# Row sums of squared differences: eight neighbouring rows on a partition, and the first load of x in two

## The chip, the cores and the metric

The kernel runs on one core of a Trainium2 chip; the other cores are idle. The metric is the device time of one execution in microseconds. "The span" of a profile is the time from its first to its last instruction, and is a little shorter than that.

The engines that matter here are VectorE (DVE in the profile), ScalarE (ACT) and SyncE (SP), whose queue issues the loads and stores. The loads themselves are carried by the core's sixteen DMA engines.

## The reference

```python
def setup_inputs():
    batch, dim = 1024, 4096
    return {
        "x": np.random.randn(batch, dim).astype(np.float32),
        "y": np.random.randn(batch, dim).astype(np.float32),
        "axis": -1,
    }

def reference(x, y, axis):
    return np.sum((x - y) ** 2, axis=axis).astype(np.float32)
```

Two arrays of 16 MiB each are read once, and 1024 sums (4 KB) are written.

## The kernel before

Each of the 128 partitions holds eight rows, 32,768 columns of x and as many of y (`N = R * D` with `R = 8`, `D = 4096`). The buffers `X` and `Y` have room for six rows, `H = 6 * D`; the last two rows go to the places of rows 0 and 1 once these are squared. Rows 0 to 3 of a partition come from the first half of the batch and rows 4 to 7 from the second.

```python
    M = N // 2
    xv = x.rearrange("(h p r) d -> p h (r d)", h=2, p=P)
    yv = y.rearrange("(h p r) d -> p h (r d)", h=2, p=P)
    ov = out.rearrange("(h p r) -> h p r", h=2, p=P)
    ...
    xw = [16384, 8192, 5472, 1280, 960, 320, 160]
    yw = [16384, 8064, 2624, 2784, 1344, 480, 480, 288]
    late, last = 128, 192
    LATE = 5
    halved = (1, 2, 3, 4)
    cut = (LATE + 1) * D - late
```

`xw` and `yw` are the widths of the loads in columns; each load moves so many columns of all 128 partitions, in one packet per partition. The loads of y leave out 128 columns at the end of row `LATE`; these come last of all, after the last 192 columns of row 7. x and y loads are put in one order, so that each load of y follows the loads of x that it needs, and SyncE's queue issues them in this order. The first two are issued ahead of the rest of the program (`prog.early`), the next ones up to the room of the buffers at once, and the others when row 1 has been squared:

```python
    todo = list(order)
    for _ in range(2):
        load(*todo.pop(0))
    prog.early(mybir.EngineType.SP)
    while todo and todo[0][5] <= H:
        load(*todo.pop(0))
```

For each load of y that has landed, VectorE subtracts piece by piece (a piece lies within one row, and the loads in `halved` are cut in two once more), and ScalarE squares and sums the piece into a column of `parts` or `results`:

```python
    def sub(c0, c1):
        a = X[:, home(c0, c1)]
        nc.vector.tensor_sub(out=a, in0=a, in1=Y[:, home(c0, c1)]).then_inc(diffs, 1)
        n["diffs"] += 1

    def square(c0, c1, acc):
        a = X[:, home(c0, c1)]
        nc.scalar.wait_ge(diffs, n["diffs"])
        nc.scalar.activation(out=a, in_=a, func=Square, accum_out=acc).then_inc(acts, 1)
        n["acts"] += 1
```

The last piece is subtracted, squared and summed on VectorE alone; its sum starts from what the rest of its row gave (`scalar`). `complete(r)` adds up the parts of row r. The first half of the results is stored once row 3 is done, the second at the end.

```python
    for j, (c0, c1) in enumerate(ys):
        final = j == len(ys) - 1
        wait_loaded(c1, landed_y[j][1])
        for piece in pieces_of(j, c0, c1):
            sub(*piece)
            r = piece[0] // D
            if final:
                nc.vector.wait_ge(diffs, n["diffs"])
                nc.vector.tensor_tensor_reduce(
                    ...
                    scalar=where[piece],
                    op0=mult,
                    op1=add,
                    accum_out=results[:, r : r + 1],
                ).then_inc(sums, 1)
                n["sums"] += 1
                continue
            square(*piece, where[piece])
            squared[piece] = n["acts"]
            if r in (0, 1):
                nc.sync.wait_ge(acts, n["acts"])
                ...                      # loads into the places of rows 0 and 1
            if r == R // 2 - 1:
                nc.sync.wait_ge(acts, n["acts"])
                nc.sync.dma_start(out=ov[0], in_=results[:, 0 : R // 2]).then_inc(stored, 16)
        if j == 4:
            for r in (4, 5, 6):
                complete(r)
            nc.vector.wait_ge(sums, n["sums"])
    complete(7)

    nc.sync.wait_ge(sums, n["sums"])
    nc.sync.dma_start(out=ov[1], in_=results[:, R // 2 : R]).then_inc(stored, 16)
```

Of the kernel before, what the change touches and what calls it, by code (L numbers as in the profile page):

```python
# [47 lines left out]
def kernel(tc, x, y, axis, out):  # L48
    nc = tc.nc
    P = nc.NUM_PARTITIONS  # L50
    F32 = mybir.dt.float32
    Square = mybir.ActivationFunctionType.Square
    mult, add = mybir.AluOpType.mult, mybir.AluOpType.add

    B, D = x.shape
    R = B // P
    N = R * D

    M = N // 2
    xv = x.rearrange("(h p r) d -> p h (r d)", h=2, p=P)
    yv = y.rearrange("(h p r) d -> p h (r d)", h=2, p=P)
    ov = out.rearrange("(h p r) -> h p r", h=2, p=P)


    H = 6 * D
    X = nc.alloc_sbuf_tensor("X", [P, H], F32).ap()
    Y = nc.alloc_sbuf_tensor("Y", [P, H], F32).ap()
    results = nc.alloc_sbuf_tensor("results", [P, R], F32).ap()  # L70

    xw = [16384, 8192, 5472, 1280, 960, 320, 160]
    yw = [16384, 8064, 2624, 2784, 1344, 480, 480, 288]
    late, last = 128, 192
    LATE = 5
    halved = (1, 2, 3, 4)
    cut = (LATE + 1) * D - late
    assert sum(xw) == N and sum(yw) == N - late - last  # L80
    xs, c = [], 0
    for w in xw:
        xs.append((c, c + w))
        c += w
    ys, c = [], 0
    for w in yw:
        ys.append((c, c + w))
        c += w
        if c == cut:
            c += late  # L90
    ys += [(N - last, N), (cut, cut + late)]

    prog = Program(nc, tc)
    stored = nc.alloc_semaphore("stored")
    diffs = prog.semaphore("diffs")
    acts = prog.semaphore("acts")
    sums = prog.semaphore("sums")
    n = dict(diffs=0, acts=0, sums=0)

    def home(c0, c1):  # L100
        h0 = c0 % H
        return slice(h0, h0 + c1 - c0)


    landed_x, landed_y = [], []
    freed = []

    def load(landed, src, dst, name, c0, c1):
        sem = prog.semaphore("%s%d" % (name, len(landed)))
        nc.sync.dma_start(out=dst[:, home(c0, c1)], in_=src[:, c0 // M, c0 % M : c0 % M + c1 - c0]).then_inc(sem, 16)  # L110
        landed.append(((c0, c1), sem))

    order = []
    have = 0
    for c0, c1 in ys:
        while have < c1:
            order.append((landed_x, xv, X, "x") + xs[len([o for o in order if o[3] == "x"])])
            have = order[-1][5]
        order.append((landed_y, yv, Y, "y", c0, c1))
# [9 lines that stand above are left out]
    row_parts = [[] for _ in range(R)]  # L129
    def pieces_of(j, c0, c1):  # L130

        pieces = []
        while c0 < c1:
            e = min(c1, (c0 // D + 1) * D)
            if j in halved:
                h = (c0 + e) // 64 * 32
                pieces.append((c0, h))
                c0 = h
            pieces.append((c0, e))
            c0 = e  # L140
        return pieces

    for j, (c0, c1) in enumerate(ys):
        for piece in pieces_of(j, c0, c1):
            row_parts[piece[0] // D].append(piece)
    parts, where = None, {}
    total = sum(len(p) for p in row_parts if len(p) > 1)
    parts = nc.alloc_sbuf_tensor("parts", [P, total], F32).ap()
    k = 0
    for r, p in enumerate(row_parts):  # L150
        for piece in p:
            where[piece] = parts[:, k : k + 1] if len(p) > 1 else results[:, r : r + 1]
            k += len(p) > 1
    first = {}
    k = 0
    for r, p in enumerate(row_parts):
        if len(p) > 1:
            first[r] = k
            k += len(p)

    def parts_of(r, m):
        return parts[:, first[r] : first[r] + m]

    seen_x = [0]

    def wait_loaded(c1, ysem):

        waits = []
        while seen_x[0] < len(xs) and xs[seen_x[0]][0] < c1:
            waits.append(seen_x[0])  # L170
            seen_x[0] += 1
        nc.vector.wait_ge(ysem, 16)
        for k in waits:
            nc.vector.wait_ge(landed_x[k][1], 16)
# [12 lines that stand above are left out]
    squared = {}  # L187

    def complete(r):

        done = row_parts[r][:-1] if r == LATE else row_parts[r]
        nc.vector.wait_ge(acts, squared[done[-1]])
        nc.vector.tensor_reduce(  # L193
            out=where[row_parts[r][-1]] if r == LATE else results[:, r : r + 1],
            in_=parts_of(r, len(done)),
            axis=mybir.AxisListType.X,
            op=add,
        ).then_inc(sums, 1)
# [11 lines that stand above are left out]
                    out=Y[:, home(*piece)],  # L210
                    in0=X[:, home(*piece)],
                    in1=X[:, home(*piece)],
                    scale=1.0,
                    scalar=where[piece],
                    op0=mult,
                    op1=add,
                    accum_out=results[:, r : r + 1],
# [8 lines that stand above are left out]
                while todo and todo[0][5] <= H + (r + 1) * D:  # L226
                    load(*todo.pop(0))
                if r == 1:
                    while todo:
                        load(*todo.pop(0))  # L230
            if r == R // 2 - 1:

                nc.sync.wait_ge(acts, n["acts"])
                nc.sync.dma_start(out=ov[0], in_=results[:, 0 : R // 2]).then_inc(stored, 16)
        if j == 4:
            for r in (4, 5, 6):
                complete(r)
            nc.vector.wait_ge(sums, n["sums"])
    complete(7)

    nc.sync.wait_ge(sums, n["sums"])
    nc.sync.dma_start(out=ov[1], in_=results[:, R // 2 : R]).then_inc(stored, 16)
    prog.close(nc.sync, stored, 32)


# [33 lines left out]
```

## Time and profile before

| | before |
|---|---|
| time, median of 3 runs | 85.02 us (84.97 to 85.23) |
| span of the profiled execution | 83.6 us |
| VectorE busy | 36.9 us (44%) |
| ScalarE busy | 33.5 us (40%) |
| moved by the DMA engines | 33.56 MB in 2736 packets, 401 GB/s over the span |

A line of the profile that begins with a line number (L178 is the subtraction, L184 the square, L193 `complete`, L209 the last squared sum, L110 the loads, L225, L234 and L242 waits or stores on SyncE's queue) gives the engine, the operation, output<-inputs with their shapes, and a count. Idle time before an instruction is in square brackets, with what ended it. "SPq" is the issuing of DMAs by SyncE's queue; how long a transfer is under way from its issue stands in the list of DMA issues. Two things count where the engines are idle half of the time: when each load lands, and what waits for it.

### The profile page before, as it was taken

How to read it: one execution, taken by the hardware profiler on the slowest of the kernel's cores; microseconds unless marked ns; L12 is line 12 of the kernel's file. 1: busy time of each engine (PE TensorE's matmuls, PEld its weight loads, DVE VectorE, ACT ScalarE, POOL GpSimd, SP SyncE). 2: the span in 40 equal slices, each digit the busy share in tenths (PEclk: the TensorE clock that was granted, in tenths of full speed). 3: DMA queues.
4: the chain of work that ended last, by engine and by line, in shares of the span. 5: the costliest groups of instructions: out<-in, count | busy, mean ns of one | idle time of the engine just before them, and what ended most of it. 6: DMA issues, size and time to landing. Idle time of an engine off the chain costs nothing.

```text
span 83.6 us, 136 instructions
## 1 busy us (share of the span) xinstructions
DVE 36.9 (44%) x27; ACT 33.5 (40%) x41; POOL 0.2 (0%) x4
## 2 busy tenths in 40 slices
DVE  0000000000000000000399999999199995989980
ACT  0500000000000000000001979797979999799980
POOL 0000000000000000000000000000000000000000
DMA  9389999975999999299979988997999899999920
GB/s 470 157 376 501 501 501 501 501 313 219 470 501 501 501 501 439 125 439 501 439 313 501 501 359 386 494 494 324 410 429 440 371 437 433 405 421 407 388 74 1
DMA packets 2736, 33.56 MB, mean 401 GB/s; under 512 B 560, under 2 KB 1456, under 8 KB 1840
## 3 DMA queue, kind: packets, MB, share of 16 engines
q1 hardware_dynamic: 2736, 33.56, 94.9%
HBM read 33.55 MB, written 0.00 MB: 401 GB/s over the span
## 4 chain that ended last, share of the span: by engine, by line
DMA 64%; SPq 17%; DVE 12%; ACT 4%; issue 1%
DMA Y<-in_y_dram 64%; SPq L110 17%; DVE X L178 11%; ACT X L184 4%; DVE Y L209 0%; DVE results L193 0%; SPq L225 0%; DVE results L209 0%
## 5 line engine op out<-in xcount | busy, mean ns | idle before, releaser
L178 DVE TENSOR_TENSOR X<-X,Y 128x4096 f32<-128x4096 f32 (+10 forms) x21 | 36.2, 1779 | 44.5 <-DMA Y<-in_y_dram 44.3
L184 ACT ACTIVATE X<-X 128x4096 f32<-128x4096 f32 (+9 forms) x20 | 31.2, 1559 | 45.8 <-DVE X L178 45.6
L184 ACT ACTIVATION_READ_ACCUMULATOR X<-X 128x1 f32 x20 | 3.7, 186 | 0.0
L184 ACT ACT_TABLE_LOAD x1 | 1.3, 1283 | 1.9 <-PEq L19 1.9
L193 DVE TENSOR_REDUCE results<-parts 128x1 f32<-128x2 f32 (+2 forms) x3 | 0.4, 151 | 0.0
L209 DVE CUSTOM_DVE_ANT_0 Y<-X,parts 128x128 f32<-128x128 f32 x1 | 0.4, 352 | 0.0
L193 DVE TENSOR_REDUCE parts<-parts 128x1 f32<-128x2 f32 x1 | 0.1, 145 | 0.0
L260 POOL MEMSET const-bfloat16-1.0<- 128x1 bf16 x1 | 0.1, 102 | 0.0
L260 POOL MEMSET const-uint8-127<- 128x1 uint8 x1 | 0.1, 102 | 0.0
L260 POOL MEMSET const-float32-0.0<- 128x1 f32 x1 | 0.1, 99 | 0.2 <-issue 0.2
L260 POOL MEMSET const-float32-1.0<- 128x1 f32 x1 | 0.1, 99 | 0.0
L209 DVE DVE_READ_ACCUMULATOR2_ANT results<- 128x1 f32 x1 | 0.1, 84 | 0.0
## 6 DMA issues: line engine op xcount, KB each, us to landing
X<-in_x_dram SPq DMA_DIRECT2D x1, 4096.0 KB, 48.9
Y<-in_y_dram SPq DMA_DIRECT2D x1, 4032.0 KB, 58.1
X<-in_x_dram SPq DMA_DIRECT2D x1, 2736.0 KB, 13.3
Y<-in_y_dram SPq DMA_DIRECT2D x1, 1392.0 KB, 18.9
Y<-in_y_dram SPq DMA_DIRECT2D x1, 1312.0 KB, 16.0
Y<-in_y_dram SPq DMA_DIRECT2D x1, 672.0 KB, 21.0
X<-in_x_dram SPq DMA_DIRECT2D x1, 640.0 KB, 19.9
X<-in_x_dram SPq DMA_DIRECT2D x1, 480.0 KB, 21.7
```

What stands on the lines that cost most here:

```text
L110: nc.sync.dma_start(out=dst[:, home(c0, c1)], in_=src[:, c0 // M, c0 % M : c0 % M + c1 - c0]).then_inc(sem, 16)
L178: nc.vector.tensor_sub(out=a, in0=a, in1=Y[:, home(c0, c1)]).then_inc(diffs, 1)
L184: nc.scalar.activation(out=a, in_=a, func=Square, accum_out=acc).then_inc(acts, 1)
L193: nc.vector.tensor_reduce(out=where[row_parts[r][-1]] if r == LATE else results[:, r : r + 1], in_=parts_of(r, len(done)), axis=mybir.Axis ...
L209: nc.vector.tensor_tensor_reduce(out=Y[:, home(*piece)], in0=X[:, home(*piece)], in1=X[:, home(*piece)], scale=1.0, scalar=where[piece], o ...
L260: nc = _bacc.Bacc("TRN2", target_bir_lowering=False, num_devices=1)
```

## The change

The map of rows to partitions becomes the plain one: partition p holds rows 8p to 8p+7, 128 KB in one run. The first load of x is split in two, 4096 columns (16 KB of each partition) and then 12288, so that the first packets are small. With the plain map, the columns that come last are now the end of row 3, and the widths of the first two y loads follow from that; row 3 has only one other part, from which the last sum can start without a reduction. The results are stored once, at the end.

```diff
-    M = N // 2
-    xv = x.rearrange("(h p r) d -> p h (r d)", h=2, p=P)
-    yv = y.rearrange("(h p r) d -> p h (r d)", h=2, p=P)
-    ov = out.rearrange("(h p r) -> h p r", h=2, p=P)
+    xv = x.rearrange("(p r) d -> p (r d)", p=P)
+    yv = y.rearrange("(p r) d -> p (r d)", p=P)
+    ov = out.rearrange("(p r) -> p r", p=P)
...
-    xw = [16384, 8192, 5472, 1280, 960, 320, 160]
-    yw = [16384, 8064, 2624, 2784, 1344, 480, 480, 288]
+    xw = [4096, 12288, 8192, 5472, 1280, 960, 320, 160]
+    yw = [16256, 8192, 2624, 2784, 1344, 480, 480, 288]
     late, last = 128, 192
-    LATE = 5
+    LATE = 3
...
-        nc.sync.dma_start(out=dst[:, home(c0, c1)], in_=src[:, c0 // M, c0 % M : c0 % M + c1 - c0]).then_inc(sem, 16)
+        nc.sync.dma_start(out=dst[:, home(c0, c1)], in_=src[:, c0:c1]).then_inc(sem, 16)
...
     def complete(r):
-        done = row_parts[r][:-1] if r == LATE else row_parts[r]
-        nc.vector.wait_ge(acts, squared[done[-1]])
+        nc.vector.wait_ge(acts, squared[row_parts[r][-1]])
         nc.vector.tensor_reduce(
-            out=where[row_parts[r][-1]] if r == LATE else results[:, r : r + 1],
-            in_=parts_of(r, len(done)),
+            out=results[:, r : r + 1],
+            in_=parts_of(r, len(row_parts[r])),
...
-                    scalar=where[piece],
+                    scalar=parts_of(r, 1),
...
-            if r == R // 2 - 1:
-                nc.sync.wait_ge(acts, n["acts"])
-                nc.sync.dma_start(out=ov[0], in_=results[:, 0 : R // 2]).then_inc(stored, 16)
         if j == 4:
             for r in (4, 5, 6):
                 complete(r)
-            nc.vector.wait_ge(sums, n["sums"])
     complete(7)
 
     nc.sync.wait_ge(sums, n["sums"])
-    nc.sync.dma_start(out=ov[1], in_=results[:, R // 2 : R]).then_inc(stored, 16)
-    prog.close(nc.sync, stored, 32)
+    nc.sync.dma_start(out=ov, in_=results).then_inc(stored, 16)
+    prog.close(nc.sync, stored, 16)
```

## The prediction

> **What bounds the kernel now.** I read the page first: its line of busy engines, the two lines of DMA and the chain that ended last.
>
> ```profile
> span 83.6 us, 136 instructions
> DVE 36.9 (44%) x27; ACT 33.5 (40%) x41; POOL 0.2 (0%) x4
> ...
> DMA packets 2736, 33.56 MB, mean 401 GB/s; under 512 B 560, under 2 KB 1456, under 8 KB 1840
> ...
> q1 hardware_dynamic: 2736, 33.56, 94.9%
> ...
> DMA Y<-in_y_dram 64%; SPq L110 17%; DVE X L178 11%; ACT X L184 4%; DVE Y L209 0%; DVE results L193 0%; SPq L225 0%; DVE results L209 0%
> ```
>
> No compute engine is busy for half of the span, and the packets of the loads fill 94.9% of the sixteen DMA engines: 0.949 x 83.6 = 79.3 us. The work is a stream of 33.55 MB, and the kernel is that stream plus a start and a tail. Next the list of DMA issues, whose last column is the time from issue to landing (the two 8 MB loads are listed without a size).
>
> ```profile
> X<-in_x_dram SPq DMA_DIRECT2D x1, 4096.0 KB, 48.9
> Y<-in_y_dram SPq DMA_DIRECT2D x1, 4032.0 KB, 58.1
> ...
> X<-in_x_dram SPq DMA_DIRECT2D x1, 21.8
> Y<-in_y_dram SPq DMA_DIRECT2D x1, 40.7
> ```
>
> With the issue times of the timeline (0.00, 0.43, 1.92 and 2.29 us) these four land at 21.8 (x), 41.1 (y), 50.8 (x) and 60.4 us (y). They were all issued in the first 3 us and arrive in the order of issue. The rate comes from the table by stretches of time, which puts a packet into the stretch in which it starts; its last two columns are the DMA share and GB/s.
>
> ```profile
> 1.00:1.25 0.25, 0.00 (x0) 0.00 (x0) 0.00 (x0) 1.00 9.42 3146
> ...
> 28.00:29.00 1.00, 0.00 (x0) 0.00 (x0) 0.00 (x0) 1.00 2.42 1049
> 45.00:46.00 1.00, 1.00 (x2) 0.41 (x1) 0.00 (x0) 1.00 1.23 524
> ```
>
> In 28 to 29 us 1049 KB start, which is sixteen packets of 64 KB, one for each engine, and their time is 2.42 us each: 65,536 B / 2.42 us = 27.1 GB/s an engine, 433 GB/s for sixteen. At 45 us sixteen packets of 32 KB take 1.23 us each, against 1.21 for half of 2.42: an additional packet costs some 0.02 us at most. In 1.00 to 1.25 us twelve packets start and take 9.42 x 0.25 x 16 / 12 = 3.14 us each: the first packet is 0.72 us longer than later ones.
>
> A model with one constant then holds for the landings: 2.4 us + bytes of one engine / 27.1 GB/s. An engine carries eight partitions of each load, so 8 x 2.42 = 19.4 us for each of the first two and 9.7 and 9.5 us for the next two: 21.8, 41.1, 50.8, 60.3 against 21.8, 41.1, 50.8, 60.4 seen. For all bytes (2.097 MB an engine, 77.4 us) it gives 79.8 us; the last load landed at 80.30. So the thirteen smaller loads lost about 0.5 us altogether, 0.04 us each.
>
> Last the timeline of VectorE, which shows how close compute is behind the stream:
>
> ```profile
> 41.13 17.43 DVE L178 TENSOR_TENSOR X<-X,Y 128x4096 f32<-128x4096 f32 x4 [41.13 <-DMA Y<-in_y_dram]
> 60.43 8.76 DVE L178 TENSOR_TENSOR X<-X,Y 128x2048 f32<-128x2048 f32 x4 [1.87 <-DMA Y<-in_y_dram]
> 70.13 2.96 DVE L178 TENSOR_TENSOR X<-X,Y 128x1312 f32<-128x1312 f32 x2 [0.94 <-DMA Y<-in_y_dram]
> 73.46 4.80 DVE L178 TENSOR_TENSOR X<-X,Y 128x736 f32<-128x736 f32 x6 [0.37 <-DMA Y<-in_y_dram]
> ...
> 78.49 2.39 DVE L178 TENSOR_TENSOR X<-X,Y 128x480 f32<-128x480 f32 x5
> 80.92 0.35 DVE L209 CUSTOM_DVE_ANT_0 Y<-X,parts 128x128 f32<-128x128 f32 x1
> ```
>
> VectorE waits for y at every stage (1.87, 0.94 and 0.37 us), and in the last stage it still has about 0.1 us of wait before each of the last two loads. The last load sets the end: landing 80.30, two subtractions 0.57, the squared sum 0.35, the reduction of row 7, then the store, issued at 81.46 and landed 2.2 us later. Another 85.02 - 83.6 = 1.4 us lie outside the span.
>
> **What the Trainium skill says.** Three places bear on it, all in "DMA: Bandwidth & Descriptors". The section "Where 436 GB/s comes from" puts the ceiling of the sixteen ports at 435.2 GB/s; the 433 GB/s of the 64 KB packets agree, so nothing in the middle of the stream is left to win. The section "Why small descriptors are slow (HBM only)" says that each packet carries a small fixed cost; the trace agrees in that 32 KB packets take 1.23 us instead of 1.21. The section "Latency and other measured facts" reports copies between HBM tensors that slow down when the row pitch is a large power of two: 207 GB/s at a pitch of 512 KiB against 214 when padded, and half of that at 4 MiB. The change doubles a pitch that is a power of two, from 64 to 128 KB, which is still below the smallest one the page has. The trace of before has the 64 KB pitch alone and runs at the ceiling, so it can't say what 128 KB does.
>
> **The change, part by part.**
>
> 1. *The map of rows.* A partition reads eight rows in one run of 128 KB instead of two runs of 64 KB half a batch apart. Bytes and packet sizes of each load stay as they were; only HBM addresses move: neighbouring partitions are 128 KB apart. The engines' rate is at their ceiling, and I take the new pitch as neutral: 0.0 us.
>
> 2. *The first load of x in two.* One load of eight 64 KB packets an engine becomes eight of 16 KB and eight of 48 KB. That is eight data packets and one completion more on each engine. At 0.04 us for an additional load (the thirteen small ones) to 8 x 0.02 us (the difference of 32 KB packets) it costs 0.04 to 0.16 us; I take +0.1. It feeds no instruction earlier: VectorE's first subtraction needs y, which is still one load of 16,256 columns, behind all 16,384 of x.
>
> 3. *What goes out early.* The first two loads in the order are issued ahead of everything else. These are now both halves of x (8.4 MB, about 19 us of stream), and y follows about 1.9 us after the first. The stream can't run dry: 0.0 us.
>
> 4. *Which end comes last.* 128 columns of row 3, instead of row 5, wait to the end. The first y load is 128 columns shorter: 65.5 KB / 433 GB/s = 0.15 us. VectorE starts at 41.13 - 0.15 + 0.1 = 41.1 us. The second y load is 128 columns longer, so the sum up to it is the same and it lands at 60.4 + 0.1 us. There VectorE has 128 columns more: the 1984-column pieces took 2.22 us and the 2048-column ones 2.29, so two of them add 0.14 us, against a wait of 0.94 us at the next stage. None of it reaches the end.
>
> 5. *The reductions.* The last piece's squared sum starts from row 3's single partial instead of the reduction of row 5. There are still three reductions (rows 4, 5 and 6), so only the wait for their completion goes. In the timeline the third of them ends at 78.45 and the next subtraction starts at 78.49: at most 0.04 us, and VectorE then waits for a load anyway. 0.0 us.
>
> 6. *One store instead of two.* The early store of the first half was issued at 71.04 us, after the last load, and landed at 80.6. It leaves the queue behind the loads, so its going frees nothing ahead of them. The last store has 32 B a partition instead of 16, in the same number of packets: I take the same 2.2 us.
>
> Sum: 0.0 + 0.1 + 0.0 + 0.0 + 0.0 + 0.0 = +0.1 us. Against it stands the rival at the start, to which I give one chance in three of about -0.3 us, that is -0.1. Together 85.02 + 0.1 - 0.1 = 85.0 us.
>
> **The rivals.**
>
> *Smaller first packets shorten the start.* The constant of 2.4 us holds 0.72 us by which the first packets are longer. If part of that grows with the packet, as when writing begins only after much of a packet is read, 16 KB packets would save up to 0.5 us: 84.5 us. For it: the cost is there, before any engine is up to speed. Against it: the late starters in the same table begin between 1.75 and 2.25 us and end with the others, so this looks like a latency that all share, which a smaller packet doesn't lower. A gain could come through: VectorE's waits of 0.37 + 0.1 + 0.1 us in the last stages are about 0.5 us that an earlier stream can still remove.
>
> *The new pitch slows reading.* If partitions 128 KB apart fall on the same parts of the memory more often, each packet gets longer. One per cent on 77.4 us is 0.8 us: 85.8 us. For it: the pages' warning on pitches. Against it: the 64 KB pitch is a power of two as well and runs at 433 of 435 GB/s, limited by the engines.
>
> *The end of the stream.* [...]From 79 to 80 us the engines move 317 GB/s with a share of 1.03. If the last few loads get a tenth slower or faster over about 2 us, that is 0.2 us either way.
>
> *Compute takes over the end.* VectorE would have to lose more than 0.9 us in the middle. The change adds 0.14 us: 85.0 us as before.
>
> **Range and chances.** The range is 84.4 to 85.7: below it would need the whole start-up gain plus a faster end (0.5 + 0.1), above it a slow-down of the stream by nearly one per cent (0.7 of 77.4 us). Two per cent are 1.7 us. To win them would need over twice the whole 0.72 us that the first packets lose; to lose them the stream would have to run 2.2% slower everywhere, which only the pitch could do. So faster 0.02, same 0.95, slower 0.03.
>
> **What would show it right or wrong.** Right: packets again 2736 (144 more for the load, 144 fewer for the store); the first part of x landing at 2.4 + 4.8 = 7.2 us, the second near 21.8, the first y near 41.0 and the last y near 80.4; packets of 48 KB at about 1.8 us; waits of VectorE of about 1.9, 0.8 and 0.4 us. The start is refuted as neutral if all landings from x on are earlier by the same few tenths. The pitch is refuted as neutral if 64 KB packets of y take clearly more than 2.42 us, so that the delay grows from landing to landing. The prediction is wrong if either moves the last landing by over 0.6 us, or if VectorE no longer waits for the last loads.

## The result, and the profile after

The changed kernel takes 84.11 us (median of 4 runs, 83.95 to 84.14) where the kernel before takes 85.12 us (84.97 to 85.55, with one more run than in the table of before): a ratio of 0.9869, 95% interval 0.983 to 0.9909. It is faster by about 1.0 us, and lies below the range of the prediction.

The page of the changed kernel begins as that of before did; the lines below are its span, its busy engines and its packets.

```profile
span 82.8 us, 136 instructions
DVE 36.9 (45%) x27; ACT 33.5 (40%) x41; POOL 0.2 (0%) x4
...
DMA packets 2736, 33.56 MB, mean 405 GB/s; under 512 B 432, under 2 KB 1328, under 8 KB 1712
```

The busy times are the same and the packets as many. Next come three lines of the list of DMA issues, with the size and the time from issue to landing, and three of the table by stretches of time (last columns: DMA share, GB/s).

```profile
Y<-in_y_dram SPq DMA_DIRECT2D x1, 8128.0 KB, 39.1
X<-in_x_dram SPq DMA_DIRECT2D x1, 6144.0 KB, 21.3
...
X<-in_x_dram SPq DMA_DIRECT2D x1, 2048.0 KB, 7.2
```

```profile
1.00:1.25 0.25, 0.00 (x0) 0.00 (x0) 0.00 (x0) 1.00 4.19 852
...
8.00:9.00 1.00, 0.00 (x0) 0.00 (x0) 0.00 (x0) 1.00 1.81 786
...
28.00:29.00 1.00, 0.00 (x0) 0.00 (x0) 0.00 (x0) 1.00 2.40 1040
```

The two parts of x land at 7.2 and 21.8 us and y at 1.9 + 39.1 = 41.0 us. The packets of 65,024 bytes in 28 to 29 us take 2.40 us each, 27.1 GB/s an engine, as the 64 KB packets did with the old map. The first packets of 16 KB (thirteen start in 1.00 to 1.25 us) take 4.19 x 0.25 x 16 / 13 = 1.29 us, about 0.68 us more than 16 KB at that rate: nearly the 0.72 us of the 64 KB packets.

VectorE's timeline has the same waits (in brackets) as before, within 0.3 us:

```profile
40.99 17.30 DVE L176 TENSOR_TENSOR X<-X,Y 128x4096 f32<-128x4096 f32 x4 [40.99 <-DMA Y<-in_y_dram]
60.43 8.90 DVE L176 TENSOR_TENSOR X<-X,Y 128x2048 f32<-128x2048 f32 x4 [2.14 <-DMA Y<-in_y_dram]
70.07 2.96 DVE L176 TENSOR_TENSOR X<-X,Y 128x1312 f32<-128x1312 f32 x2 [0.74 <-DMA Y<-in_y_dram]
73.40 4.80 DVE L176 TENSOR_TENSOR X<-X,Y 128x736 f32<-128x736 f32 x6 [0.37 <-DMA Y<-in_y_dram]
```

So the stream hardly moved. The last thing ahead of the store is the reduction of row 7, which waits for ScalarE's square of that row's last 192 columns. It starts 0.03 us (unrounded) after ScalarE's last instruction has ended, at 81.05 + 0.18 = 81.23 us before and at 80.93 + 0.19 = 81.12 us after. The profile's chain puts the end down to the last waited-for load instead, as the prediction did; VectorE's work behind that load ended at nearly the same time. First before, then after:

```profile
81.05 0.18 ACT L184 ACTIVATION_READ_ACCUMULATOR X<-X 128x1 f32 x1
...
81.27 0.16 DVE L193 TENSOR_REDUCE results<-parts 128x1 f32<-128x8 f32 x1
```

```profile
80.93 0.19 ACT L182 ACTIVATION_READ_ACCUMULATOR X<-X 128x1 f32 x1
...
81.15 0.16 DVE L189 TENSOR_REDUCE results<-parts 128x1 f32<-128x8 f32 x1
```

And these are the last store's issue and, from the answer on its line, its time to landing; again first before, then after:

```profile
81.46 0.34 SPq L242 DMA_DIRECT2D out_dram<-results  x1
...
DMA to landing us min/median/max: 2.2/2.2/2.2
```

```profile
81.34 0.35 SPq L233 DMA_DIRECT2D out_dram<-results  x1
...
DMA to landing us min/median/max: 1.4/1.4/1.4
```

Of the 0.85 us between the profiled spans, 0.06 us are there when the subtractions of 736 columns begin (the timeline's last line, 73.46 and 73.40 us), 0.06 come from there to the store's issue (8.00 and 7.94 us), and 0.73 from the store itself (landed after 2.15 and 1.42 us). The trace has the landing of each of the sixteen engines; for four transfers these are the first and the last engine's, in us from the start. The lower two rows are two later runs, on a chip with the number 9.

```
kernel, chip            first 16384 of x   first y        last load      last store
before, first           21.23 to 21.79     40.62 to 41.10  80.13 to 80.48  82.70 to 83.61
changed, first          21.40 to 21.77     40.60 to 40.97  80.25 to 80.47  82.58 to 82.76
before, chip 9          21.36 to 21.94     40.81 to 41.31  80.15 to 80.59  82.82 to 82.99
changed, chip 9         21.35 to 21.90     40.56 to 41.09  80.08 to 80.47  82.66 to 82.83
```

In the first measurement the store of the kernel before begins to land after 1.2 us, as the others do, but its engines then come in over 0.9 us instead of 0.2.

### The profile page after: what moved, and what is told of

Read it like the earlier page. It is cut to its first block, busy times and chain, and to the rows that moved or that the text cites. A ratio compares the mean times of both kernels' runs of the same rounds, so it can differ in the third digit from the quotient of the medians.

```text
span 82.8 us, 136 instructions
## 1 busy us (share of the span) xinstructions
DVE 36.9 (45%) x27; ACT 33.5 (40%) x41; POOL 0.2 (0%) x4
## 2 busy tenths in 40 slices
DMA packets 2736, 33.56 MB, mean 405 GB/s; under 512 B 432, under 2 KB 1328, under 8 KB 1712
## 3 DMA queue, kind: packets, MB, share of 16 engines
q1 hardware_dynamic: 2736, 33.56, 96.0%
## 4 chain that ended last, share of the span: by engine, by line
DMA 63%; SPq 16%; DVE 12%; ACT 4%; issue 1%
DMA Y<-in_y_dram 63%; SPq L108 16%; DVE X L176 11%; ACT X L182 4%; DVE Y L205 0%; DVE results L189 0%; SPq L221 0%; DVE results L205 0%
## 5 line engine op out<-in xcount | busy, mean ns | idle before, releaser
L176 DVE TENSOR_TENSOR X<-X,Y 128x2048 f32<-128x2048 f32 (+10 forms) x21 | 36.2, 1779 | 44.4 <-DMA Y<-in_y_dram 44.2
L182 ACT ACTIVATE X<-X 128x2048 f32<-128x2048 f32 (+9 forms) x20 | 31.2, 1559 | 45.7 <-DVE X L176 45.7
## 6 DMA issues: line engine op xcount, KB each, us to landing
Y<-in_y_dram SPq DMA_DIRECT2D x1, 8128.0 KB, 39.1
```

## The experiments

My theory after the result was that the last store's packets of 16 bytes land later than packets of 32. The rivals: the early store into the same output slows the last one; the map or the split of x makes the gain; or the slow store belongs to the chip of that measurement. Each experiment was run beside the kernel before on one chip. The record of the first measurement doesn't name its chip; the others have numbers.

| kernel | chip | us | before there | ratio, 95% interval |
|---|---|---|---|---|
| b_store32 | 12 | 84.40 | 84.34 | 1.0011 (0.9996 to 1.0025) |
| b_noearly | 12 | 84.40 | 84.34 | 1.0014 (1.0002 to 1.0026) |
| a_store16 | 12 | 84.68 | 84.34 | 1.0048 (1.0035 to 1.006) |
| a_unsplit | 12 | 84.21 | 84.34 | 0.9989 (0.9977 to 1.0001) |
| before_again | 9 | 84.31 | 84.33 | 0.9992 (0.9982 to 1.0002) |
| after_again | 9 | 84.04 | 84.33 | 0.9965 (0.9951 to 0.9978) |
| b_split | 9 | 84.18 | 84.33 | 0.9986 (0.9977 to 0.9995) |
| before_look | 4 | 84.20 | 84.34 | one run |
| b_noearly_2 | 4 | 84.34 | 84.34 | 1.0002 (0.9993 to 1.0011) |
| a_half16 | 4 | 84.10 | 84.34 | 0.9972 (0.9963 to 0.9981) |
| a_fine | 4 | 84.36 | 84.34 | 1.0003 (0.9995 to 1.0012) |
| b_noearly_3 | 5 | 84.30 | 84.37 | 0.9995 (0.9981 to 1.0008) |
| after_3 | 7 | 84.14 | 84.34 | 0.9974 (0.9964 to 0.9983) |
| a_unsplit_2 | 7 | 84.12 | 84.34 | 0.9978 (0.9966 to 0.9989) |
| b_split_2 | 7 | 84.18 | 84.34 | 0.9986 (0.997 to 1.0003) |
| b_noearly_4 | 7 | 84.39 | 84.34 | 1.0014 (0.9993 to 1.0036) |
| a_oldmap | 9 | 84.30 | 84.34 | 0.9995 (0.998 to 1.0009) |
| a_unsplit_3 | 9 | 84.24 | 84.34 | 0.9988 (0.9979 to 0.9997) |

The kernel before needs 84.33 to 84.37 us on all five chips, 0.8 us less than in the first measurement. The changed kernel needs 84.04 and 84.14 us, as it did there.

### The last store

**One store of 32 bytes in the kernel before.** The output's order differs from the reference's here, because each partition's results go to eight neighbouring places.

```diff
-                nc.sync.dma_start(out=ov[0], in_=results[:, 0 : R // 2]).then_inc(stored, 16)
...
-    nc.sync.dma_start(out=ov[1], in_=results[:, R // 2 : R]).then_inc(stored, 16)
-    prog.close(nc.sync, stored, 32)
+    nc.sync.dma_start(out=out.rearrange("(p r) -> p r", p=P), in_=results).then_inc(stored, 16)
+    prog.close(nc.sync, stored, 16)
```

> The kernel before with one edit: both stores are replaced by one at the end, of 32 bytes per partition (each partition's eight results go to eight neighbouring places of the output, so the output's order differs from the reference's). Loads and map are those of before. If the packet size of the last store makes the difference: the store lands about 1.4 us after its issue instead of 2.2, and the time is about 84.2 us. If the split of x or the map of the loads makes it: 85.0 to 85.1 us and 2.2 us.

**No early store.** Rows 0 to 3 of each partition are not written.

```diff
-            if r == R // 2 - 1:
-                nc.sync.wait_ge(acts, n["acts"])
-                nc.sync.dma_start(out=ov[0], in_=results[:, 0 : R // 2]).then_inc(stored, 16)
...
-    prog.close(nc.sync, stored, 32)
+    prog.close(nc.sync, stored, 16)
```

> The kernel before without its early store (rows 0 to 3 of the output are not written); the last store keeps its 16 bytes per partition. If the packet size of the last store makes the difference: nothing changes, 85.0 to 85.1 us, store landing in 2.2 us. If an earlier store into the same output slows the last one: about 84.2 us and 1.4 us.

**The changed kernel's store in packets of 16 bytes.**

```diff
-    results = nc.alloc_sbuf_tensor("results", [P, R], F32).ap()
+    results = nc.alloc_sbuf_tensor("results", [P, 2 * R], F32).ap()
...
-    nc.sync.dma_start(out=ov, in_=results).then_inc(stored, 16)
+    nc.sync.dma_start(
+        out=out.rearrange("(p a b) -> p a b", p=P, a=2),
+        in_=results.rearrange("p (a b) -> p a b", a=2)[:, :, 0:4],
+    ).then_inc(stored, 16)
```

> The changed kernel with one edit: the results lie in two groups of four with a gap, so that its single store goes out in 256 packets of 16 bytes instead of 128 of 32. If the packet size makes the difference: the store takes about 2.2 us or somewhat more and the time is 84.9 to 85.1 us. If the early store, the map or the split makes it: 84.1 to 84.2 us, with the store landing in 1.4 to 1.5 us.

All three ran on chip 12. With packets of 32 bytes the time is that of the kernel before, and without the early store it is that or 0.1 us more. The store in 16-byte packets without an early one lands in 1.4 us, as its line in the list of DMA issues shows:

```profile
out_dram<-results SPq DMA_DIRECT2D x1, 2.0 KB, 1.4
```

The store of 256 packets of 16 bytes does cost something, 84.68 against 84.21 us for the changed kernel with the whole first load. Its issue and its line in the list of DMA issues:

```profile
81.37 0.62 SPq L233 DMA_DIRECT2D out_dram<-results  x1
...
out_dram<-results SPq DMA_DIRECT2D x1, 4.0 KB, 1.9
```

From issue to landing it takes 1.9 us instead of 1.4; 0.27 us of the difference are a longer issue (0.62 against 0.35 us). Its engines land within 0.2 us of each other (83.14 to 83.31), so this isn't what happened in the first measurement: twice as many packets cost it, not their size. So my theory had nothing to explain on this chip, and the next question was whether the kernel before was slow at all elsewhere.

**Both kernels unchanged, on one chip.**

> The kernel before, unchanged, to see how long its last store takes on the chip of this call. If the 2.2 us belong to the kernel (its packets of 16 bytes or its early store): again 2.2 us and a time 0.8 us over that of the changed kernel. If they belonged to the chip or the placement of that first measurement: 1.4 us here, and both kernels within 0.3 us of each other.

> The changed kernel, unchanged, on the same chip as the kernel before. If the gain belongs to the kernel: 0.9 to 1.0 us faster than before, as in the first measurement. If it came from a slow store of the kernel before on that chip alone: 0.1 to 0.3 us faster, with the store landing in 1.4 us in both.

On chip 9 the store of the kernel before takes 1.4 us. The first of these lines is from the timeline, the second from the answer on the store's line:

```profile
81.58 0.34 SPq L242 DMA_DIRECT2D out_dram<-results  x1
...
DMA to landing us min/median/max: 1.4/1.4/1.4
```

The changed kernel is 0.3 us faster there, not 1.0. That fits the third rival: 0.7 us of the first measurement are its own. Whether they belong to its chip or to the occasion is not shown.

**In search of a chip like the first.** If packets of 16 bytes or the early store are slow only on some chips, it takes such a chip to tell them apart. Five runs were made for that: four with two kernels shown above (the kernel before, and it without the early store), and a fifth of the changed kernel that stores only rows 4 to 7 of each partition, in 16-byte packets that are 32 bytes apart.

```diff
-    nc.sync.dma_start(out=ov, in_=results).then_inc(stored, 16)
+    nc.sync.dma_start(out=ov[:, R // 2 : R], in_=results[:, R // 2 : R]).then_inc(stored, 16)
```

> The kernel before, unchanged, for another look at its last store. If the 2.2 us from issue to landing belong to some chips: either 2.2 us with a time near 85.0, or 1.4 us with a time near 84.3, and the time of the kernel before on this chip goes with it. If the first measurement was a single chance: 1.4 us and 84.3 us.

> The kernel before without its early store (rows 0 to 3 of the output are not written). On a chip where the kernel before needs 2.2 us for the last store: still 2.2 us if packets of 16 bytes are what is slow there, 1.4 us if the early store is. On a chip where it needs 1.4 us: 1.4 us and 84.3 us, no difference.

> The changed kernel, which stores only rows 4 to 7 of each partition (16 bytes a packet, 32 bytes apart; rows 0 to 3 of the output are not written). On a chip where the kernel before needs 2.2 us for the last store: 2.2 us if packets of 16 bytes are slow there, 1.4 us if it is the early store or packets of 16 bytes side by side. Elsewhere 1.4 us and 84.0 to 84.1 us.

> The kernel before without its early store (rows 0 to 3 of the output are not written), tried on another chip in search of one where the kernel before needs 85.0 us. There: about 85.0 us with the store landing in 2.2 us if its packets of 16 bytes are what is slow, 84.3 us and 1.4 us if the early store is. On a chip where the kernel before needs 84.3 us: 84.3 us and 1.4 us, which tells nothing more.

> The kernel before without its early store (rows 0 to 3 of the output are not written). On a chip where the kernel before needs 85.0 us: 85.0 us and a store of 2.2 us if packets of 16 bytes are slow there, 84.3 us and 1.4 us if the early store is. Elsewhere the same as before, 84.3 us and 1.4 us.

Chips 4, 5 and 7 are as 9 and 12: the kernel before near 84.3 us, the last store landing in 1.4 us in all five profiles, and packets of 16 bytes no slower than of 32 (a_half16 keeps the changed kernel's lead). None was like the first, so what was slow there stays open.

### What remains: the split, and the rest

**The split alone.**

```diff
-    xw = [16384, 8192, 5472, 1280, 960, 320, 160]
+    xw = [4096, 12288, 8192, 5472, 1280, 960, 320, 160]
```

> The kernel before with the first load of x in two (4096 and 12288 columns) and nothing else. If an additional load only costs: 0 to 0.1 us slower than before, as predicted. If the small first packets shorten the start: all landings earlier by up to 0.3 us and the time with them.

> The kernel before with the split alone. If the split gives about half: 0.1 to 0.15 us faster than before. If all: 0.3 us faster. If nothing: no difference, or 0.1 us slower for the additional load.

**All but the split.** The changed kernel with this line taken back.

```diff
-    xw = [4096, 12288, 8192, 5472, 1280, 960, 320, 160]
+    xw = [16384, 8192, 5472, 1280, 960, 320, 160]
```

> The changed kernel with the first load of x whole again (16384 columns in 64 KB packets). If the split does nothing, as the landing of the last load (80.23 against 80.30 us) suggests: 84.0 to 84.2 us, first y near 40.9 us. If the split shortens the start: up to 0.5 us longer, 84.6 us, all landings later by as much.

> The changed kernel with the first load of x whole. If the split gives about half of the 0.3 us: 0.1 to 0.15 us faster than before. If the split gives all of it: no difference from before. If it gives nothing: 0.3 us faster, as the changed kernel.

> The changed kernel with the first load of x whole and the new map, beside the old map: 0.1 to 0.2 us faster than before, as on the two chips so far. If it is no faster here, the difference is the chips' own and not the kernel's.

**The changed kernel once more, on the chip of b_split_2 and a_unsplit_2.**

> The changed kernel beside its two halves on one chip: 0.3 us faster than before (ratio near 0.9965) if the gain seen on the second chip holds; 1.0 us faster only on a chip where the kernel before needs 85.0 us.

By the ratios, the split alone gives 0.12 us on both chips, though on chip 7 the interval reaches 1. All but the split gives 0.1, 0.2 and 0.1 us on chips 12, 7 and 9 (on chip 12 the interval reaches 1), and both together 0.3 and 0.2 us on chips 9 and 7. On chip 7 the changed kernel without the split is as fast as with it (84.12 and 84.14 us). The parts are of the same size, 0.1 to 0.2 us each, and only roughly add up. In the first profile of the split, on chip 9, VectorE's first wait ends 0.28 us earlier than in the kernel before on that chip, and the later ones 0.27 to 0.30; first before, then with the split:

```profile
41.33 17.43 DVE L178 TENSOR_TENSOR X<-X,Y 128x4096 f32<-128x4096 f32 x4 [41.33 <-DMA Y<-in_y_dram]
```

```profile
41.05 17.43 DVE L178 TENSOR_TENSOR X<-X,Y 128x4096 f32<-128x4096 f32 x4 [41.05 <-DMA Y<-in_y_dram]
```

The engine that lands first has y at 40.81 and 40.67 us, the one that lands last at 41.31 and 41.03: the slowest engine gained twice as much as the fastest. But this profile overstates it: it caught the fastest of the thirteen executions (84.07 us), and in the second profile of the split (chip 7) the first y lands at 41.19 us.

**A finer split.**

```diff
-    xw = [4096, 12288, 8192, 5472, 1280, 960, 320, 160]
+    xw = [1024, 3072, 12288, 8192, 5472, 1280, 960, 320, 160]
```

> The changed kernel with the first load of x in three: 1024, 3072 and 12288 columns (first packets of 4 KB). If the gain of the split grows as the first packets get smaller: the slowest engine lands another 0.1 to 0.2 us earlier, 83.9 us where the changed kernel has 84.05. If the first small packets are all that is to be had: 84.0 to 84.1 us; if additional loads cost 0.1 us each: 84.15 us.

It takes 84.36 us, where a_half16, the same loads with the split in two, takes 84.10 on the same chip. Smaller first packets don't help: going from two loads to three costs 0.26 us. Whether the third load or the packets of 4 KB cost it is not told apart. The fastest engine has its first y at 40.60 us, against 40.57 in a_half16; the slowest at 41.28 against 41.15.

**The map alone taken back.** The changed kernel with the whole first load and the loads in the map of before; its output's order differs from the reference's.

```diff
-    xw = [4096, 12288, 8192, 5472, 1280, 960, 320, 160]
+    xw = [16384, 8192, 5472, 1280, 960, 320, 160]
...
-    xv = x.rearrange("(p r) d -> p (r d)", p=P)
-    yv = y.rearrange("(p r) d -> p (r d)", p=P)
+    M = N // 2
+    xv = x.rearrange("(h p r) d -> p h (r d)", h=2, p=P)
+    yv = y.rearrange("(h p r) d -> p h (r d)", h=2, p=P)
...
-        nc.sync.dma_start(out=dst[:, home(c0, c1)], in_=src[:, c0:c1]).then_inc(sem, 16)
+        nc.sync.dma_start(out=dst[:, home(c0, c1)], in_=src[:, c0 // M, c0 % M : c0 % M + c1 - c0]).then_inc(sem, 16)
```

> The changed kernel with the first load of x whole and the loads in the old map (two runs of 64 KB half a batch apart), storing 32 bytes per partition, so that the output's order differs from the reference's. If the map of the loads makes the remaining 0.2 us: no difference from before. If the end of row 3 instead of row 5, with its reduction and wait, makes it: 0.1 to 0.2 us faster than before, as with the new map.

It is at 0.9995, beside 0.9988 for the new map in the same comparison. The intervals overlap: a difference of 0.06 us is below what these runs can tell. That the new map is worth something is not shown; that it costs no more than 0.1 us is.

**How the kernel ends, in all twenty profiles.** What VectorE and ScalarE do from the subtractions of 736 columns on is called the last stages here. They always begin 0.02 us after their y has landed. In the ten profiles whose last columns are the end of row 5 (the kernel before and its variants), the first subtraction of 480 columns comes 5.02 to 5.03 us after this beginning and the issue of the last store 7.99 to 8.00 us, although the last load lands anywhere from 6.94 to 7.02 us after it. In the ten profiles with the end of row 3 they come 4.91 to 4.96 and 7.87 to 7.98 us after it. In all twenty the reduction of row 7 starts 0.03 us after ScalarE's last instruction has ended, while it starts 0.02 to 0.17 us after VectorE's own instruction before it. So from this beginning on it is compute that sets the end of the kernel before, and not the last loads. On chip 4 (before_look) the profile's own chain has it so:

```profile
79.15 2.06 ACT X L184 x8
...
81.24 0.16 DVE results L193
```

What the changed kernel saves there begins at the reductions of rows 4 to 6. Before, the next subtraction waits for the third of them (started at 78.31, ended at 78.45) and starts at 78.49 us. In the changed kernel it starts ahead of the third one's end at 78.12 + 0.27 = 78.39 us:

```profile
78.12 0.27 DVE L189 TENSOR_REDUCE results<-parts 128x1 f32<-128x2 f32 x3
...
78.36 2.46 DVE L176 TENSOR_TENSOR X<-X,Y 128x480 f32<-128x480 f32 x5
```

On chip 9, before_again and a_unsplit_3 begin the last stages at 73.58 and 73.59 us; from there to the store's issue they take 7.99 and 7.90 us. The 0.09 us are the size of what all but the split gives on that chip. Where the last loads are waited for, part of the gain is lost (7.98 us in a_unsplit). No run takes back the wait for the reductions alone, so that it makes all of the rest is not shown.

No version tried is clearly faster than the changed kernel.

## Why the prediction was wrong

**The step that failed** is the sixth, "I take the same 2.2 us" for the last store. It took 1.4 us, which is 0.73 of the 0.85 us between the two profiled spans. I had read the 2.2 us off one profile and treated them as a property of the store. On chips 9 and 4 the same instruction of the same kernel took 1.4 us, and on chips 12, 5 and 7 the kernel's time agrees with that. Had I known that, I would still not have predicted the first measurement: no experiment has reproduced its slow store, and why the changed kernel escaped it is open. The change of packet size and the missing early store are both candidates there. On the chips tried, b_store32 and the four runs without the early store show that neither is worth anything.

**The split** (step 2) was taken as a cost of 0.1 us; it is a gain of about 0.1. The rival at the start had the right sign, and its weight of one in three was too small, but its mechanism is not what the trace shows: the first packets of 16 KB carry the same 0.7 us as those of 64 KB, so this latency isn't what the split shortens. What it shortens isn't settled; in one profile the slowest engine gains most. One term of the cost was misread: the 0.02 us for an additional packet came from a single microsecond of the table. In the next one, from 46 to 47 us, the same 32 KB packets take 1.21 us, and all 128 of them have a median of 1.213, 0.003 more than half of 2.42.

**The end** (the reading "The last load sets the end", step 5, and the rival "Compute takes over the end") was wrong, too. Step 5 put 0.0 us on the reductions because VectorE then waits for a load anyway. But ScalarE, close behind VectorE, set the end of the kernel before without any change, and the missing wait for the reductions let the next subtraction start up to 0.12 us sooner (5.03 to 4.91 us). The store was then issued 0.01 to 0.13 us sooner after the same landing.

**The rival on the pitch** is refuted for this kernel: 64 KB packets run at 27.1 GB/s with either map, the landings grow no delay, and all but the split is a little faster than before.

**What held.** Packets (2736), the first parts of x (7.2 and 21.8 us), the first y (41.0), packets of 48 KB (1.81 us) came as worked out. In the first y there is luck: the +0.1 us in it had the wrong sign, and in the changed kernel's three profiles it landed at 40.97, 41.09 and 41.12 us. The last waited-for landing, read as 80.4, was 80.23 us; the load behind it landed at 80.47 and no instruction had to wait for it. VectorE's waits of 1.9, 0.8 and 0.4 us were 2.14, 0.74 and 0.37. The 128 more columns in the second stage cost 0.14 us (8.90 against 8.76) and didn't reach the end. Steps 3 and 4 were of no weight. The change of time stayed below the two per cent that the prediction called the same. On the two other chips on which the changed kernel ran, the sum of the steps (+0.1 us) was off by 0.3 to 0.4 us: about 0.2 are the split (from +0.1 to -0.1), and the rest is of the size of the shorter end.

## What to carry to other kernels

When a kernel is a saturated stream, the stream's own landings can be worked out to 0.1 or 0.2 us, and what is uncertain lies at its two ends: the moment at which the slowest engine starts, and the last store's landing. A time read off one profile at such an end is one draw: before it enters a sum as a constant, look at the same instruction on another chip, and compare a small change with the kernel before on several chips. Where compute runs close behind the last loads, a profile's chain names one path of two that end almost together; find out which engine's last instruction the final one really follows, at the same distance in every profile. Splitting the first load in two was worth about 0.1 us here, and going on to three lost 0.26, so such a step has to be measured.

## What the runs showed of the hardware

The sixteen engines don't land alike, and most of the difference stays. On chip 4 the kernel before has its first and last engine's landings 0.60 us apart at the first x (21.23 to 21.83), 0.58 at the first y (40.58 to 41.16), 0.57 at the second y (59.86 to 60.43) and 0.55 at the 192 columns near the end (79.67 to 80.22): most of the lag is there at the first landing. It can also shrink: in the first measurement it went from 0.56 to 0.35 us before and from 0.37 to 0.22 in the changed kernel. (The landings aren't named by engine; that it is the same one that lags is inferred from the nearly constant distance.) In the profiles of this case that distance at the first y lies between 0.36 and 0.71 us, which is more than any part of this change is worth.

In the running stream a packet's time goes with its size: 64, 48, 32 and 16 KB take 2.42, 1.81, 1.21 and 0.61 us in the median. The first packets take about 0.7 us more, with 16 KB (0.68) as with 64 KB (0.72).

A store of 2 KB was landed in 1.4 us on five chips, and in 2.2 us in the first measurement, where its engines came in over 0.9 us instead of 0.2.
